# Opening the SSD stage while the last half sums run, and putting the dt products behind the column tiles in the first-phase blocks, in a two-layer hybrid kernel

## The chip, the cores and the metric

The kernel runs on one core of one Trainium2 chip. The metric is the device time of one execution in microseconds (us); lower is better. Engines are named as the profile names them: PE (TensorE, matmuls), DVE (VectorE), ACT (ScalarE), POOL (GpSimd) and SP (SyncE, which here issues nearly all DMAs).

## The reference, cut to what matters

Three tiles of 128 tokens (one of context, two of latents) pass through two layers. Layer 0 is the one the change touches. Its input is normalised and modulated, and one wide projection feeds two mixers; mixer B is a bidirectional Mamba-2 scan (SSD).

```python
ss, scs, gs = modulation(c, mod_w[layer], mod_b[layer])       # Linear(SiLU(cond)), split in three
hs = rms_norm(xs, norm_pre[layer]) * (1 + scs) + ss
...
p = h @ w_in                                                  # u, v, za | z | x, B, C | dt
...
xbc = jax.nn.silu(depthwise_conv(xbc, conv_w, conv_b))        # 5 taps, centred
dt = jax.nn.softplus(dt_raw.reshape(b, n, 2, B_HEADS) + dt_bias)
a = -jnp.exp(a_log)
y_f, h_f = ssd_scan(xs, dt[:, :, 0], a[0], bm, cm, h0_f)
y_b, h_b = ssd_scan(flip(xs), flip(dt[:, :, 1]), a[1], flip(bm), flip(cm), h0_b)
y = y_f + flip(y_b) + (d_skip[0] + d_skip[1])[:, None] * xs
y = y.reshape(b, n, B_WIDTH) * jax.nn.silu(z)
y = rms_norm(y.reshape(b, n, B_GROUPS, B_WIDTH // B_GROUPS), ...)
```

There are 32 heads of 64 channels in 8 groups, with a state of 128 and chunks of 128 tokens.

## The kernel before

Every weight is cut into units of 128 x 1024 (512 KB) in the order of use, and each float32 product is made of three matmuls: a unit is split into a high part `wh` (ACT) and the rest `wl` (DVE), the activations into `hH` and `hL`, and PE adds `hH*wh`, `hL*wh` and `hH*wl`. A list `plan` holds all units in order. SP loads them into three `raw` buffers; `wh` and `wl` have four buffers each, so a split waits until PE has used the unit four places earlier.

The order of all instructions is fixed when the program is built. A model clock (`Clock`) guesses when each engine is free; generators hold the side work (convolution, scan, gates), and after each triple of matmuls `tick()` lets those go on whose inputs the clock holds ready. At the end `in_order` ties each engine to that written order. On the chip nothing is moved: an instruction that waits holds up all that stand behind it on its engine.

**First phase (the `while` loop after `x_in`).** The modulation weights come in eight blocks `b` of eight units. `mod_pair` multiplies two units by the condition (rows `sm<-aL,sc` and `sm<-wide,sc`); after the fourth pair ACT copies the sum (`rb`), PE makes columns of it (`sm<-sel,rb`), and DVE and ACT make two more 128-row blocks of `hb`, `hH` and `hL`, the modulated input. Only then can products with these rows start. One unit per block, `part`, holds the weights of four column tiles (group 0 of x, B and C); its products go to the four banks of `first`. One unit holds all weights of dt, split into `dth`; its products go to a fifth bank, `dt_ps`. Ten units called `half` are half sums of later column tiles (groups 1 to 3), rows `sm<-hH,wh` and the like; they need the first four blocks and are parked in SBUF rows `r`.

**SSD stage.** `dt_gen` turns `dt_ps` into decays; `conv_gen(g, i)` runs the convolution of column tile `i` (0, 1: x, 2: B, 3: C) of group `g`; `ssd_gen` is the scan, `decay_gen` the decay matrices (rows `EE`, `cb`), `gate_gen` the gate and the norm of one group. Meanwhile PE makes the projections of the next columns. PSUM has eight banks: five for products (`mm`), three for the side work (`sm`). A product needs a free `mm` bank:

```python
pss = [bank() for _ in range(NT)]        # three banks: the z columns of two groups
xstat(pss, hH, hL, k1=8)                 # first half of the rows
xbc(2 * q)                               # four column tiles, one bank each
xstat(pss, hH, hL, k0=8)                 # second half
spawn(zs_gen(q, pss))
xbc(2 * q + 1)
```

The bank of a column tile is free when `conv_gen` has copied it out (rows `xpad<-mm,r` on DVE or `xpad<-mm` on ACT). The three z banks are free when `zs_gen` has read them (ACT `zs<-mm`, then DVE `zs<-zs,mm`); `zs` has one buffer, so this waits until the gate of the group before has made its last product with the old `zs` (DVE `v<-v,zs`) and ACT has taken its square (`tmp,ss<-v`). Column tile `i` of group `g` is called (g, i) below. Groups 0 to 3 with q up to 1 are the part that matters here.

Of the kernel before, what the change touches and what calls it, by code (L numbers as in the profile page):

```python
# [16 lines left out]
P = 128  # L17
# [158 lines left out]
def build(tc, A, O):  # L176
# [5 lines left out]
    with ExitStack() as ctx:  # L182
# [223 lines left out]
        for b in range(8):  # L406
            many, at = SIDE.get(b, (0, 0))
            for u in range(8):
                if b > 0 and u == at:
                    if b == 1:  # L410
                        job(("dt",), "w", "win0", 0)
                    job(("part", b - 1), "w", "win0", b)
                    for _ in range(many):
                        job_half()
                job(("mod", b, u), "raw", "mod0", 8 * b + u)
# [158 lines left out]
        convw = pd.tile([P, 32, 6], F32, name="convw")  # L574
        st = ExitStack()
# [112 lines left out]
        def weights(n):  # L688
# [13 lines left out]
            if what[0] == "part":  # L702
                hv = h.rearrange("p (k i c) -> p k i c", k=2, i=4)
                lv = l.rearrange("p (k i c) -> p k i c", k=2, i=4)
                for kk in range(2):
                    k = 2 * what[1] + kk
                    q.append((k, (dthl[:, k],), lambda k=k: dt_one(k)))
                    for i in range(4):
                        q.append(product(first[i][:, :T], hv[:, kk, i], lv[:, kk, i], k, k == KC - 1))
                q.append((None, (), close_w))  # L710
            else:
# [20 lines left out]
        def ready(item):  # L732
            k, aps, _ = item
            if k is None:
                return 0.0
            if k // 2 not in rows_of_h:
                return None
# [31 lines left out]
        while mod_at or w_at or rb or any(queue.values()):  # L769
# [22 lines left out]
            if what == "x":  # L792
                x_transpose(*xts.pop(0))
                if not xts:
                    stx.close()
                    wide = pool("wide", 1, st=stx, side="right").tile([P, 6, UNIT], F32, name="wide")
                    more += [wide[:, i] for i in range(6)]
                    dt_ps = bank()
                    first = [bank() for _ in range(4)]
            elif what == "rb":  # L800
# [3 lines left out]
                if b == 1:  # L804
                    SP.dma_start(out=convw, in_=A["convw"])
            elif what == "mod":
# [22 lines left out]
        assert len(part) == len(half) + 4 and not held.keys() & set(range(phase))  # L829
        state["next"] = phase  # L830
# [17 lines left out]
        dsk2 = pd.tile([P, 2, 32], F32, name="dsk2")  # L848
        dsk = pd.tile([P, 32], F32, name="dsk")
        arow = pd.tile([P, 64], F32, name="arow")  # L850
        dtb = pd.tile([P, 64], F32, name="dtb")
        S.dma_start(out=dsk2, in_=A["dskip"].partition_broadcast(P))
        S.dma_start(out=arow, in_=A["alog"].partition_broadcast(P))
        S.dma_start(out=dtb, in_=A["dtbias"].partition_broadcast(P))
# [338 lines left out]

        spawn(dt_gen())
        for i in range(4):
            spawn(conv_gen(0, i, None))
        spawn(ssd_gen())
# [695 lines left out]
```

## Time and profile before

| | us |
|---|---|
| median of three runs | 1825.82 (1821.43 to 1825.92) |
| the profiled execution, its own time | 1825.12 |
| its span, first to last instruction | 1823.3 |
| PE busy in the span | 1771.7 (97%) |
| DVE, ACT, POOL busy | 1258.9, 739.5, 202.2 |

The span is divided by the profile into busy and idle time of each engine, and idle time is put down to the engine or the DMA that ended it. Since PE is busy for 97% of the span, what counts is the 51.6 us in which it is not. All instructions are recorded by one helper, so the line is L155 everywhere, and rows are told apart by their tiles.

### The profile page before, as it was taken

How to read it: one execution, taken by the hardware profiler on the slowest of the kernel's cores; microseconds unless marked ns; L12 is line 12 of the kernel's file. 1: busy time of each engine (PE TensorE's matmuls, PEld its weight loads, DVE VectorE, ACT ScalarE, POOL GpSimd, SP SyncE). 2: the span in 40 equal slices, each digit the busy share in tenths (PEclk: the TensorE clock that was granted, in tenths of full speed). 3: DMA queues.
4: the chain of work that ended last, by engine and by line, in shares of the span. 5: the costliest groups of instructions: out<-in, count | busy, mean ns of one | idle time of the engine just before them, and what ended most of it. 6: DMA issues, size and time to landing. Idle time of an engine off the chain costs nothing.

```text
span 1823.3 us, 24950 instructions
## 1 busy us (share of the span) xinstructions
PE 1771.7 (97%) x9319; PEld 1542.9 (85%) x9319; DVE 1258.9 (69%) x2024; ACT 739.5 (41%) x1380; POOL 202.2 (11%) x247
## 2 busy tenths in 40 slices
PE   6899999999999999999999999998999999999998
PEld 3579888989998788889999999877789898988876
DVE  4335787787668777777888788666477676876444
ACT  3224665565543422333333323245434444444441
POOL 0000242243211000000000000021301010000000
PEclk9999999999999999999999999999999999999999
DMA  9883555455434565676666666685464444444483
GB/s 358 349 317 118 177 156 157 137 153 166 133 116 152 183 217 169 221 223 207 202 215 202 198 210 206 206 255 193 136 196 151 144 148 136 152 141 140 148 274 116
DMA packets 109896, 340.89 MB, mean 187 GB/s; under 512 B 11984, under 2 KB 29904, under 8 KB 108624
## 3 DMA queue, kind: packets, MB, share of 16 engines
q1 hardware_dynamic: 109248, 339.18, 56.9%
q8 instruction: 73, 1.20, 0.3%
q14 instruction: 47, 0.39, 0.1%
q10 hardware_dynamic: 528, 0.13, 0.0%
HBM read 330.22 MB, written 9.04 MB: 186 GB/s over the span
## 4 chain that ended last, share of the span: by engine, by line
PE 67%; DVE 5%; DMA 3%; ACT 2%; issue 2%; POOL 1%; DVEq 0%; POOLq 0%; ACTq 0%; SPq 0%
PE mm L155 62%; PE sm L155 5%; DMA raw<-in_wout_dram 2%; DVE wl L155 1%; DVE acc L155 1%; ACT jk L155 1%; ACT wh L155 1%; DVE hb L155 1%; DVE v L155 1%; DMA raw<-in_mod_dram 0%; DVE out L155 0%; DMA gn<-gate 0%; DVE cs L155 0%; DMA raw<-in_win_dram 0%; ACT xn L155 0%
## 5 line engine op out<-in xcount | busy, mean ns | idle before, releaser
L155 DVE TENSOR_TENSOR wl<-raw,wh 128x1024 fp32r<-128x1024 f32 x358 | 439.6, 1235 | 297.1 <-ACT wh L155 294.9
L155 ACT ACTIVATE wh<-raw 128x1024 fp32r<-128x1024 f32 x358 | 376.0, 1056 | 489.5 <-DMA raw<-in_win_dram 205.7
L155 PE MATMUL mm<-hH,wh 128*128 128x384 f32 x1200 | 422.3, 352 | 4.2 <-DVE xpad L155 4.2
L155 PE MATMUL mm<-hH,wl 128*128 128x384 f32 x1200 | 403.8, 337 | 1.4 <-DVE wl L155 1.4
L155 PE MATMUL mm<-hL,wh 128*128 128x384 f32 x1200 | 403.1, 336 | 0.0
L155 DVE SCALAR_TENSOR_TENSOR acc<-raw,scol,acc 128x512 f32<-128x512 f32 x480 | 336.8, 762 | 12.8 <-DMA raw<-in_mod_dram 12.5
L155 PE MATMUL mm<-wh,hH 128*128 128x512 f32 x636 | 261.5, 411 | 0.8 <-ACT v L155 0.8
L155 PE MATMUL mm<-wh,hL 128*128 128x512 f32 x636 | 248.9, 391 | 0.6 <-POOL hL L155 0.6
L155 PE MATMUL mm<-wl,hH 128*128 128x512 f32 x636 | 248.1, 390 | 0.0
L155 PEld LDWEIGHTS mm<-hH,wh 128*128 128x128 f32 x1200 | 226.5, 189 | 23.1 <-issue 20.6
L155 PEld LDWEIGHTS mm<-hH,wl 128*128 128x128 f32 x1200 | 226.2, 189 | 2.4 <-DVE wl L155 2.4
L155 PEld LDWEIGHTS mm<-hL,wh 128*128 128x128 f32 x1200 | 226.7, 189 | 1.9
L155 PE MATMUL mm<-wh,aL 128*128 128x512 f32 x504 | 197.1, 391 | 0.0
L155 PEld LDWEIGHTS mm<-wh,hL 128*128 128x128 f32 x636 | 119.3, 188 | 26.9 <-POOL hL L155 1.1
L155 PEld LDWEIGHTS mm<-wh,hH 128*128 128x128 f32 x636 | 119.6, 188 | 25.7 <-ACT v L155 1.3
L155 PEld LDWEIGHTS mm<-wl,hH 128*128 128x128 f32 x636 | 119.8, 188 | 24.0
L155 PE MATMUL mm<-wh,r 128*128 128x512 f32 x348 | 136.9, 393 | 0.5 <-DVE out L155 0.5
L155 PE MATMUL mm<-wl,r 128*128 128x512 f32 x348 | 136.2, 391 | 0.9 <-DVE wl L155 0.9
L155 POOL TENSOR_TENSOR rs_r<-rs_t,nhalf 128x1 f32<-128x1 f32 (+1 forms) x54 | 43.0, 798 | 648.1 <-DVE rs_t L155 648.1
L155 PEld LDWEIGHTS mm<-wh,aL 128*128 128x128 f32 x504 | 95.0, 189 | 19.9
L155 DVE SCALAR_TENSOR_TENSOR cv<-xpad,convw,cv 128x386 f32<-128x386 f32 x128 | 84.3, 662 | 2.3
L155 PEld LDWEIGHTS mm<-wh,r 128*128 128x128 f32 x348 | 65.3, 188 | 16.3 <-issue 2.1
(256 smaller groups left out, 2074.8 us busy)
## 6 DMA issues: line engine op xcount, KB each, us to landing
raw<-in_win_dram SPq DMA_DIRECT2D x273, 512.0 KB, 4.0
raw<-in_mod_dram SPq DMA_DIRECT2D x128, 512.0 KB, 4.1
raw<-in_wout_dram SPq DMA_DIRECT2D x104, 512.0 KB, 4.2
aL<-in_mod_dram SPq DMA_DIRECT2D x52, 512.0 KB, 7.8
cb<-cumd SPq DMA_DIRECT2D x32, 384.0 KB, 5.2
wide<-in_mod_dram SPq DMA_DIRECT2D x12, 512.0 KB, 9.9
gn<-gate SPq DMA_DIRECT2D x8, 512.0 KB, 7.0
x<-in_x_dram SPq DMA_DIRECT2D x3, 1024.0 KB, 7.3
```

Source lines behind the costliest of these rows:

```text
L155: i = f(*a, **kw)
```

## The change

Three things move. (1) In the first block the unit of `part` is loaded and split ahead of that of dt, and in every block the eight column products of the unit stand ahead of the two dt products. (2) The loop of the first phase becomes a function, `phase_job`. It runs alone until only half sums are left; then the pools of the SSD stage are opened, `dt_gen` and the convolutions of group 0 are started, and the remaining half sums are made with a `tick()` after each job. (3) Three small loads (`dskip`, `alog`, `dtbias`) go from ACT's queue at the start of the SSD stage to SP's queue after the fifth block. No product, split or copy is added or taken away.

```diff
                 if b > 0 and u == at:
+                    job(("part", b - 1), "w", "win0", b)
                     if b == 1:
                         job(("dt",), "w", "win0", 0)
-                    job(("part", b - 1), "w", "win0", b)
...
                 for kk in range(2):
                     k = 2 * what[1] + kk
-                    q.append((k, (dthl[:, k],), lambda k=k: dt_one(k)))
                     for i in range(4):
                         q.append(product(first[i][:, :T], hv[:, kk, i], lv[:, kk, i], k, k == KC - 1))
                 q.append((None, (), close_w))
+                for kk in range(2):
+                    k = 2 * what[1] + kk
+                    q.append((k, (dthl[:, k],), lambda k=k: dt_one(k)))
...
-        while mod_at or w_at or rb or any(queue.values()):
+
+        def phase_job():
+            nonlocal first, dt_ps
             pump()
...
+                if b == 4:
+                    SP.dma_start(out=dsk2, in_=A["dskip"].partition_broadcast(P))
+                    SP.dma_start(out=arow, in_=A["alog"].partition_broadcast(P))
+                    SP.dma_start(out=dtb, in_=A["dtbias"].partition_broadcast(P))
...
+        while mod_at or rb or queue["part"] or any(jobs[n][0] != "half" for n in w_at):
+            phase_job()
         st.close()
...
         spawn(dt_gen())
         for i in range(4):
             spawn(conv_gen(0, i, None))
+        while w_at or queue["half"]:
+            phase_job()
+            tick()
         spawn(ssd_gen())
         spawn(decay_gen())
```

The first place is PE in block 0, behind the first block's columns (`sel`). The dt products stand first before the change.

```order
L155 MATMUL sm_304<-sel_83,rb_298 128x2 x4
L155 MATMUL sm_319<-aL_107,sc_125 32x512 x4
L155 MATMUL mm_277<-hH_101,dth_182 128x384
L155 MATMUL mm_277<-hL_102,dth_182 64x384
L155 MATMUL mm_278<-hH_101,wh_328 128x384
L155 MATMUL mm_278<-hL_102,wh_328 128x384
L155 MATMUL mm_278<-hH_101,wl_329 128x384
```

After the change, at the same place, the column products come first (bank `mm_282` is what `mm_278` was).

```order
L155 MATMUL sm_308<-sel_83,rb_302 128x2 x4
L155 MATMUL sm_323<-aL_107,sc_129 32x512 x4
L155 MATMUL mm_282<-hH_101,wh_330 128x384
L155 MATMUL mm_282<-hL_102,wh_330 128x384
L155 MATMUL mm_282<-hH_101,wl_331 128x384
L155 MATMUL mm_283<-hH_101,wh_330 128x384
```

All four column tiles and a pair of modulation units are now done before dt's first product, which moved some 30 matmuls down; in the later blocks too the dt products stand behind.

The second place is ACT where the first phase ends. Before the change ACT copies two of the `first` banks (`r1`, `r2`), goes on with the half sums (`r5`, `r3`), issues the three small loads, and opens the SSD stage with `arow` and the copy of `dt_ps` (`EE<-mm`).

```order
L155 ACTIVATE r2_672<-mm_280 128x384
L155 ACTIVATE wh_1149<-raw_1018 128x1024
L155 ACTIVATE r5_675<-sm_1092 128x384
L155 ACTIVATE wh_1163<-raw_1065 128x1024
L155 ACTIVATE r3_673<-sm_1162 128x384
L155 ACTIVATE wh_1195<-raw_1097 128x1024
L155 ACTIVATE r3_673<-sm_1194 128x384
L155 DMA dsk2_1240<-in_dskip_dram 128x64
L155 DMA arow_1242<-in_alog_dram 128x64
L155 DMA dtb_1243<-in_dtbias_dram 128x64
L155 ACTIVATE arow_1242<-arow_1242 128x64
L155 ACTIVATE EE_1272<-mm_277 128x384
```

After it the opening stands right behind the copies, with the first convolutions (`cv`).

```order
L155 ACTIVATE r2_679<-mm_284 128x384
L155 ACTIVATE arow_123<-arow_123 128x64
L155 ACTIVATE EE_1186<-mm_281 128x384
L155 ACTIVATE cv_1191<-xpad0_1176,convw_120 128x386
L155 ACTIVATE cv_1195<-xpad1_1177,convw_120 128x386
L155 ACTIVATE r5_682<-sm_1099 128x384
L155 ACTIVATE wh_1202<-raw_1072 128x1024
L155 ACTIVATE EE_1185<-EE_1185 128x192
L155 ACTIVATE r3_680<-sm_1201 128x384
```

On PE the first small products of dt (`sm<-EE`) moved with it: they stood behind the first 33 z products, and now stand ahead of the last 33 half-sum matmuls.

The third place is DVE and ACT at the column tiles of group 3, which PE makes behind the z columns of q = 1. Before the change the bank that PE takes for tile (3, 3) is that of tile (3, 1), `mm_2472`, and DVE frees it in the last row here (the z banks are `mm_1769` to `mm_1771`, and come free later).

```order
L155 SCALAR_TENSOR_TENSOR cv_2506<-xpad0_1247,convw_120,cv_2506 128x386 x2
L155 TENSOR_TENSOR v0_1231<-v0_1231,zs_1569 128x256
L155 TENSOR_TENSOR wl_2615<-raw_2443,wh_2614 128x1024
L155 SCALAR_TENSOR_TENSOR cs3_2644<-cs3_2644,cv_2361 128x128
L155 SCALAR_TENSOR_TENSOR cs3_2644<-cs3_2644,cv_2361 128x256
L155 TENSOR_TENSOR xpad1_1248<-mm_2472,r3_673 128x256
```

After the change PE takes the first z bank, `mm_1801`, for tile (3, 2), and the wait built into its first matmul `mm_2613<-hH_101,wh_2395` is for the last of these DVE rows; between the last matmul of tile (3, 1) and that one no PE instruction stands in the program.

```order
L155 TENSOR_TENSOR tmp_2526<-sm_2523,ec_1174 128x512
L155 TENSOR_TENSOR v0_1167<-v0_1167,tmp_2526 128x256 x2
L155 TENSOR_SCALAR v0_1167<-v0_1167,rs_r_2437 128x256
L155 TENSOR_TENSOR v0_1167<-v0_1167,sm_2540 128x256
L155 TENSOR_TENSOR v0_1167<-v0_1167,zs_1624 128x256
L155 SCALAR_TENSOR_TENSOR cv_2462<-xpad1_1177,convw_120,cv_2462 128x386 x2
L155 TENSOR_TENSOR v0_1167<-v0_1167,zs_1624 128x256
L155 TENSOR_TENSOR EE_2497<-EE_2497,cb_2329 128x3x128
L155 SCALAR_TENSOR_TENSOR cv_2390<-xpad0_1176,convw_120,cv_2390 128x386 x2
L155 TENSOR_TENSOR EE_2497<-EE_2497,cb_2421 128x3x128
L155 TENSOR_TENSOR v0_1167<-v0_1167,zs_1624 128x256
L155 SCALAR_TENSOR_TENSOR zs_2610<-zs_2610,mm_1801 128x512
```

ACT's rows of the same stretch stand like this; DVE's last row above needs the `zs<-mm` in the last row here.

```order
L155 ACTIVATE wh_2514<-raw_2354 128x1024
L155 ACTIVATE tmp_2554,ss_2553<-v0_1167 128x256
L155 ACTIVATE tmp_2563,ss_2562<-v0_1167 128x256
L155 ACTIVATE EE_2497<-cb_2421,bj_1172 128x128 x3
L155 ACTIVATE cb_2421<-cb_2421,bj_1172 128x128 x3
L155 ACTIVATE r0_2589<-sm_2585,vec_84 128x384
L155 ACTIVATE EE_2497<-cb_2498,bj_1172 128x128 x3
L155 ACTIVATE cb_2498<-cb_2498,bj_1172 128x128 x3
L155 ACTIVATE tmp_2608,ss_2607<-v0_1167 128x256
L155 ACTIVATE zs_2610<-mm_1801 128x512
```

So the eviction of the z columns moved ahead in the program, from behind tile (3, 3) to in front of tile (3, 2), and the scan, gate and decay work that it needs moved with it. From the end of the SSD stage on, PE's order is the same in both programs.

## Rows read from the trace of the kernel before

**Rows 1.** Waits of PE over the whole span: us in total, times, longest

```profile
PE mm L155 <- DVE xpad L155: 4.2, 3, 2.6
PE mm L155 <- DVE dth L155: 3.6, 1, 3.6
...
PE sm L155 <- DVE v L155: 0.8, 1, 0.8
```

**Rows 2.** Busy time by stretch: length, then PE, PEld, DVE, ACT, POOL, clock, DMA

```profile
75.00:175.00 100.00, 99.71 (x576) 80.01 (x577) 35.90 (x60) 31.12 (x44) 2.02 (x6) 0.99 0.66 242
```

**Rows 3.** Timeline of PE, block 0: start, length, row, idle time before it

```profile
33.16 0.69 PE L155 MATMUL mm<-hH,dth 128*128 128x384 f32 x1 [3.58 <-DVE dth L155]
```

**Rows 4.** Timeline of ACT, block 0

```profile
30.81 1.04 ACT L155 ACTIVATE dth<-raw 128x1024 fp32r<-128x1024 f32 x1
```

**Rows 5.** Timeline of DVE, block 0

```profile
31.88 1.23 DVE L155 TENSOR_TENSOR dth<-raw,dth 128x1024 fp32r<-128x1024 f32 x1
33.02 1.22 DVE L155 TENSOR_TENSOR wl<-raw,wh 128x1024 fp32r<-128x1024 f32 x1
```

**Rows 6.** Timeline of PE, block 3

```profile
72.62 0.44 PE L155 MATMUL mm<-hH,dth 128*128 128x384 f32 x1 [1.68 <-ACT hH L155]
...
74.83 0.69 PE L155 MATMUL mm<-hH,wl 128*128 128x384 f32 x1 [0.48 <-DVE wl L155]
```

**Rows 7.** Timeline of PE, starts of tiles (2,3), (3,0), (3,2), (3,3)

```profile
252.75 0.41 PE L155 MATMUL mm<-hH,wh 128*128 128x384 f32 x1 [0.52 <-DVE xpad L155]
...
279.23 0.53 PE L155 MATMUL mm<-hH,wh 128*128 128x384 f32 x1
...
291.05 0.41 PE L155 MATMUL mm<-hH,wh 128*128 128x384 f32 x1 [1.12 <-DVE xpad L155]
...
303.09 0.49 PE L155 MATMUL mm<-hH,wh 128*128 128x384 f32 x1 [2.58 <-DVE xpad L155]
...
304.98 1.98 PE L155 MATMUL sm<-cm,cs 128*128 128x128 f32 x9
```

**Rows 8.** Busy time by stretch behind the start of tile (3,3), columns as in rows 2

```profile
303.00:305.00 2.00, 1.91 (x7) 1.85 (x8) 0.28 (x1) 1.66 (x2) 0.00 (x0) 0.57 0.58 234
...
307.00:309.00 2.00, 2.00 (x13) 2.00 (x12) 0.00 (x0) 2.00 (x7) 0.00 (x0) 1.00 0.86 271
```

**Rows 9.** Timeline of PE, first z product and dt's first small products

```profile
164.79 0.39 PE L155 MATMUL mm<-wh,hH 128*128 128x512 f32 x1
...
172.32 0.78 PE L155 MATMUL sm<-EE 128*128 128x64 f32 x6
```

**Rows 10.** Timeline of DVE ahead of tile (3,3), to the release of the z banks

```profile
296.34 0.54 DVE L155 TENSOR_TENSOR EE<-EE,cb 128x384 f32<-128x384 f32 x1
296.81 0.41 DVE L155 TENSOR_TENSOR v<-v,zs 128x256 f32<-128x256 f32 x1
297.14 1.26 DVE L155 SCALAR_TENSOR_TENSOR cv<-xpad,convw,cv 128x386 f32<-128x386 f32 x2
298.32 0.42 DVE L155 TENSOR_TENSOR v<-v,zs 128x256 f32<-128x256 f32 x1
300.32 1.23 DVE L155 TENSOR_TENSOR wl<-raw,wh 128x1024 fp32r<-128x1024 f32 x1 [1.58 <-ACT wh L155]
...
310.16 0.69 DVE L155 SCALAR_TENSOR_TENSOR zs<-zs,mm 128x512 f32<-128x512 f32 x1 [3.40 <-ACT zs L155]
```

**Rows 11.** Timeline of ACT in the same stretch

```profile
294.32 0.97 ACT L155 ACTIVATE EE<-cb,bj 128x128 f32<-128x128 f32 x3
295.20 0.97 ACT L155 ACTIVATE cb<-cb,bj 128x128 f32<-128x128 f32 x3
...
298.83 0.42 ACT L155 ACTIVATE tmp<-v 128x256 bf16<-128x256 f32 x1 [1.07 <-DVE v L155]
...
299.25 1.04 ACT L155 ACTIVATE wh<-raw 128x1024 fp32r<-128x1024 f32 x1
```

**Rows 12.** One tile's instructions: DVE rows that read xpad, ns shortest/median/longest

```profile
L155 DVE SCALAR_TENSOR_TENSOR cv<-xpad,convw,cv x128: 522/621/977, 173.8 to 562.3; 128x386 f32<-128x386 f32 x128
```

More of the change, by code (lines that the diff above doesn't have):

```diff
@@ L574, in build @@
         convw = pd.tile([P, 32, 6], F32, name="convw")
+        dsk2 = pd.tile([P, 2, 32], F32, name="dsk2")
+        dsk = pd.tile([P, 32], F32, name="dsk")
+        arow = pd.tile([P, 64], F32, name="arow")
+        dtb = pd.tile([P, 64], F32, name="dtb")
         st = ExitStack()
@@ L735, in ready @@
                 return 0.0
+            if "dt" in [jobs[n][0] for n in w_at] and aps and aps[0].name == dthl.name:
+                return None
             if k // 2 not in rows_of_h:
@@ L796, in build @@
                     wide = pool("wide", 1, st=stx, side="right").tile([P, 6, UNIT], F32, name="wide")
-                    more += [wide[:, i] for i in range(6)]
+                    more.extend(wide[:, i] for i in range(6))
                     dt_ps = bank()
@@ L828, in build @@
                         free()
-        assert len(part) == len(half) + 4 and not held.keys() & set(range(phase))
-        state["next"] = phase
+        while mod_at or rb or queue["part"] or any(jobs[n][0] != "half" for n in w_at):
+            phase_job()
         st.close()
@@ L847, in build @@
         tot = pd.tile([P, NT, 64], F32, name="tot")
[L848 to L854, printed above, removed]
         xpad = [pw.tile([P, PADW], F32, name=f"xpad{i}") for i in range(2)]
@@ L1196, in build @@
             spawn(conv_gen(0, i, None))
+        while w_at or queue["half"]:
+            phase_job()
+            tick()
+        assert len(part) == len(half) + 4 and not held.keys() & set(range(phase))
+        state["next"] = phase
         spawn(ssd_gen())
```

## The prediction

> **What bounds the kernel.** I read the share of each engine first: PE is busy for 1771.7 of 1823.3 us, so the program is as long as PE's work plus the 51.6 us in which PE stands still, and only what adds to or takes from that idle time (or slows PE's clock) can move the end. The second view is the list of PE's waits. It names no DMA: PE waits for copies and splits on DVE and ACT [rows 1]. The third is the pace of PE where nothing holds it: 576 matmuls, nearly all of 384 columns, in 99.71 us at a granted clock of 0.99 [rows 2], so 0.173 us each. The changed program has the same matmuls, and from the end of the SSD stage on they stand in the same order. I therefore count only waits ahead of that point: the wait for dt's split (3.6 us) and those for `xpad` copies (4.2 us in three) with the small one for `v` (0.8 us), and any new wait.
>
> **Term a: the first phase, +0.4 us.** In block 0, PE stands idle for 3.58 us until 33.16, for dt's split [rows 3]. ACT's first split there starts at 30.81 and takes 1.04 [rows 4], and DVE's two follow at 31.88 and 33.02 [rows 5], 1.14 apart. With `part` first, the same two engines make the same splits in the other order. PE can then start two products (those with `wh`) at about 31.9, but the next needs `wl`, which is where dt's was, at 33.1. So the wait changes its name, and some 0.6 us of work is pulled ahead of it. I give no credit for that: the next block's products wait for the modulated rows, which come from the modulation chain and not from this unit, so PE only waits that much longer there. Blocks 1 to 7 already have their order of loads; there only PE's order changes. Behind block 3, PE started dt's products at 72.62, after 1.68 us for `hH`, and still waited 0.48 for `wl` at 74.83 [rows 6]: the two dt matmuls (2 x 0.173 = 0.35 us) lay inside a wait that ends with `wl` in any case. After the change they stand behind, so the wait is 0.35 longer and they cost their time later: +0.35, rounded with some slack to +0.4. Bounds: -1.7 if the 0.6 us head start keeps PE's clock up in block 0, +1.5 if a longer idle in block 1 takes it down once more; both sizes are what half clock costs in term b.
>
> **Term b: waits that go, -6.7 us.** Four waits belong to the old order of banks and convolutions: 0.52, 1.12 and 2.58 us at the starts of tiles (2,3), (3,2) and (3,3) [rows 7], and 0.8 for `v` [rows 1]: 5.0. The last of the three costs more than itself. Behind it six matmuls take from 303.09 to 304.98, 1.89 us [rows 7], where 6 x 0.173 = 1.04 is usual, and the nine small ones behind them 1.74 instead of some 0.9 (an estimate from half of it). The granted clock there is 0.57, and 1.00 again from 307 [rows 8]: 1.2 instead of 2.4 GHz. That is 0.85 + 0.85 = 1.7 us. All of it goes if the SSD stage is far enough ahead when PE comes there.
>
> How far ahead is it? Everything of it is opened while 33 matmuls of half sums and the 33 first z products are still to be made. The z products took from 164.79 to 172.32 [rows 9], 7.5 us, the half sums 33 x 0.173 = 5.7: a head start of 13.2 us for the side work.
>
> **Term c: waits that come, +9.7 us.** The head start makes the banks turn differently. Two places are left where PE meets a bank that is not yet free.
>
> At tile (2,3), PE takes the bank of the `xpad` copy as before. One split and one gate product more stand ahead of that copy on DVE now; I put the wait at 0.9 (before 0.52), with 0 and 1.7 (the 0.52 and one split, 1.14) as its ends.
>
> At tile (3,2), PE takes a z bank, since the program has its release in front. I walk there, with zero at the start of tile (3,1) on PE.
> - PE: (3,0) and (3,1) with the small products took from 279.23 to 289.93 (291.05 less the wait of 1.12), 10.7 us, of which 48 x 0.173 = 8.3 are tile products [rows 7]. Tile (3,1) alone is 24 x 0.173 = 4.15 and some 2.4 of small products: PE is through at 6.5, and nothing else stands in its program before the z bank.
> - DVE: by laying its rows out one behind the other I have it at the copy of the last bank of group 2 until -2.0. Then come two splits (1.14), two pairs of convolution products (297.14 to 298.32, 1.18), one `EE` product (296.34 to 296.81, 0.47), `tmp` (as the z eviction, 0.69) and six products of `v` (296.81 to 297.14, 0.33) [rows 5, 10]: 2.3 + 2.4 + 0.5 + 0.7 + 2.0 = 7.8. A split waits for ACT's half, as at 300.32, where that was 1.58 [rows 10]; I take 1.9 for both. The second gate product is there at 7.7.
> - ACT: then the square of `v` (0.42), twelve exponentials (294.32 to 295.20 is 0.88 for three, so 3.5), a copy of 128 x 384 (0.5, estimate from the 0.42 of 128 x 256), the last square (0.42) and the z activation (0.5, estimate likewise) [rows 11]. An engine keeps its order: at 298.83 ACT waited 1.07 for `v`, with a split behind it that needed no `v` [rows 11]. ACT is done at 7.7 + 5.3 = 13.0.
> - DVE's `zs` product takes 0.69 [rows 10]: the bank is free at 13.7, and PE has waited **7.2 us**.
>
> A second way to the same: before, the z banks came free at 310.16 + 0.69 = 310.85 [rows 10], 19.8 us after (3,2) had started at 291.05 [rows 7]. Less 13.2 of head start that is 6.6. The walk is the finer of the two and I keep 7.2. Its ends: 5.3 if the splits never wait for ACT (7.2 - 1.9), 9.3 if DVE runs as it does in its slow rows, 977 ns for a convolution product instead of 621 (0.36 more for each of four, and the rest in proportion) [rows 12].
>
> PE stands for 7.2 us, so I expect the half clock behind it as behind the 2.58 [rows 8], and put it at 1.5. The Trainium skill ("TensorE: Matmul & The Clock Gate", Part 1, What's actually happening) says that the throttled state is the default and that activity releases it. It speaks against this change, which swaps three short stops for one long one: by it the long stop is sure to cost a restart. It also says that there are only two rates, so that the length of the stop should not matter to the price, and that leaves the sum as it is; were the price in proportion to the stop (1.7 x 7.2 / 2.58 = 4.7), the sum would be 3.2 higher. No run here shows yet which. In all 0.9 + 7.2 + 1.5 = 9.6, and 0.1 for a short new wait in group 3's last tiles: +9.7. Behind the stall the side work has caught up, so I charge nothing at (3,3).
>
> **The small loads, 0.** Three DMA issues leave ACT, 1.4 us there by the gaps in its timeline, which was not awaited by PE; SP gets them behind the fifth block, where its own queue waits for free buffers and PE waits for no DMA. If SP's issues did delay a weight by their 1.4 us, PE would have to be short of weights, which no row of [rows 1] shows.
>
> **Sum.** 1825.12 (the profiled execution's own time, 0.7 under the median) + 0.4 - 6.7 + 9.7 = 1828.5; with the 0.7 to the median, **1829 us**. Some 0.3%, 5.5 us, is about what a measurement of this kernel can tell from no change.
>
> **Rivals.**
> 1. *The stage is early enough, and nothing waits at (3,2):* 1825.8 + 0.4 - 6.7 + 0.9 = 1820. It decides at 6.5 us behind the start of (3,1): the gate's last square must be done 7 us sooner than in my walk. For it speaks that the walk adds one engine's rows behind the other's, and that the two copies of work on ACT might be done while DVE is waiting; against it that twelve exponentials stand on ACT ahead of the release in the order printed above, and the second way (19.8 less 13.2). 0.10.
> 2. *The stall is longer:* DVE shares its time with POOL's work and runs at its slow rows, 9.3, the clock price is the proportional one or a second restart follows: 1829 + 2.1 + 1 to 3 = 1832 to 1834. For it: 977 ns in [rows 12]; against: the median of 621 holds for most. 0.25.
> 3. *The first phase decides:* a kept clock in block 0 (-1.7) with a stall at its low end (5.3): 1829 - 1.7 - 1.9 = 1825.4, no change at all. 0.10.
> 4. My forecast, 1829, with its own range of 1826 to 1831: 0.55.
>
> Faster by over 0.3% (below 1820.3) takes the lower half of rival 1 and a little of 3: 0.10. Slower by over 0.3% (above 1831.3) takes rival 2: 0.27. Within: 0.63. The range reaches from rival 1's time to past rival 2's: 1820 to 1835.
>
> **What would show it.** In the changed kernel's waits of PE: no `xpad` wait above 1 us, and one new wait of a product for DVE's `zs`, 5 to 9 us, at the start of tile (3,2), with a clock near half behind it. ACT's rows ahead of it should be twelve exponentials between two squares of `v`. In block 0 the wait for dt's split becomes one for `wl` of about 1.2 us behind two products, and behind block 3 the wait for `wl` grows by 0.35. If the `zs` wait is under 2 us, the walk has failed at the order of ACT or at the head start; if it is there and the time is still lower, the price of term b was too small.

## The result, and the profile after

The changed kernel took 1836.32 us (median of four runs, 1835.19 to 1838.64) against 1825.87 before: a ratio of 1.0061, 95% interval 1.0049 to 1.0073, so 0.6% or some 10.5 us slower. The forecast was 1829, range 1820 to 1835. The profiled execution has a span of 1835.2 us (1823.3 before). PE made the same 9319 matmuls in it and was busy 2.1 us longer (1773.8 against 1771.7):

```profile
PE 1773.8 (97%) x9319; PEld 1545.8 (84%) x9319; DVE 1261.6 (69%) x2024; ACT 738.7 (40%) x1380; POOL 206.9 (11%) x247
```

Waits of PE over the whole span (us in total, times, longest), changed kernel; the lines that stand where [rows 1] stood:

```profile
PE mm L155 <- ACT wh L155: 9.2, 6, 2.5
PE mm L155 <- DVE zs L155: 8.4, 1, 8.4
PE mm L155 <- DVE wl L155: 4.9, 9, 0.8
...
PE mm L155 <- ACT tmp L155: 3.4, 1, 3.4
...
PE sm L155 <- DVE v L155: 0.9, 1, 0.9
```

No row of the list names dt's split or an `xpad` copy on DVE any more. The 9.2 us for `wh` are no loss of that size: most of them lie in the first phase, where PE now waits for the split of the unit of `part` instead of for dt's split (3.6 us before), `hH` (2.7) and `hL` (1.7). New are a stop of 8.4 us for the z columns and one of 3.4 us that the list puts down to ACT's `tmp`. Where these two are, in the timeline of PE (start, length, row, idle time before it):

```profile
259.73 0.41 PE L155 MATMUL mm<-hH,wh 128*128 128x384 f32 x1 [3.40 <-ACT tmp L155]
...
262.54 1.80 PE L155 MATMUL sm<-xb,xw 128*128 128x128 f32 x8
264.10 0.42 PE L155 MATMUL mm<-hH,wh 128*128 128x384 f32 x1
...
298.88 0.33 PE L155 MATMUL sm<-cm,v 128*128 128x128 f32 x1 [0.89 <-DVE v L155]
307.56 0.69 PE L155 MATMUL mm<-hH,wh 128*128 128x384 f32 x1 [8.35 <-DVE zs L155]
...
311.57 0.49 PE L155 MATMUL mm<-hH,wh 128*128 128x384 f32 x1
```

The row at 259.73 is the start of tile (2,3), that at 307.56 the start of tile (3,2). Behind each the granted clock is down (length, PE, PEld, DVE, ACT, POOL, clock, DMA):

```profile
260.00:265.00 5.00, 5.00 (x25) 4.96 (x24) 3.14 (x6) 3.40 (x9) 1.23 (x2) 0.66 0.46 157
305.00:310.00 5.00, 2.44 (x8) 2.44 (x9) 2.92 (x4) 3.70 (x10) 0.00 (x0) 0.50 0.25 34
```

Behind (3,2) twelve matmuls take 4.01 us (307.56 to 311.57) where 12 x 0.173 = 2.08 is usual: 1.9 us lost. Behind (2,3) six take 1.96 us instead of 1.04 and eight small ones 1.56 (262.54 to 264.10) where the next eight of their kind take 0.81 (335.87 to 336.68): 1.7 lost.

What ended the stop at (3,2), on DVE and ACT of the changed kernel:

```profile
299.08 0.42 DVE L155 TENSOR_TENSOR v<-v,zs 128x256 f32<-128x256 f32 x1
...
300.60 0.74 DVE L155 TENSOR_TENSOR v<-v,zs 128x256 f32<-128x256 f32 x1
...
303.78 0.80 DVE L155 TENSOR_TENSOR EE<-EE,cb 128x384 f32<-128x384 f32 x1 [0.46 <-POOL cb L155]
304.50 0.41 DVE L155 TENSOR_TENSOR v<-v,zs 128x256 f32<-128x256 f32 x1
306.82 0.69 DVE L155 SCALAR_TENSOR_TENSOR zs<-zs,mm 128x512 f32<-128x512 f32 x1 [1.90 <-ACT zs L155]
```

```profile
301.85 0.97 ACT L155 ACTIVATE EE<-cb,bj 128x128 f32<-128x128 f32 x3
302.72 0.97 ACT L155 ACTIVATE cb<-cb,bj 128x128 f32<-128x128 f32 x3
303.60 0.56 ACT L155 ACTIVATE r<-sm,vec 128x384 fp32r<-128x384 f32 x1
304.06 0.97 ACT L155 ACTIVATE EE<-cb,bj 128x128 f32<-128x128 f32 x3
304.94 0.97 ACT L155 ACTIVATE cb<-cb,bj 128x128 f32<-128x128 f32 x3
305.81 0.40 ACT L155 ACTIVATE tmp<-v 128x256 bf16<-128x256 f32 x1
...
306.21 0.57 ACT L155 ACTIVATE zs<-mm 128x512 f32<-128x512 f32 x1
```

The third product of `v` is there at 304.9, but ACT is in its twelve exponentials until 305.8: the picture of the walk. The product itself stands behind an `EE` product that takes ACT's second three exponentials as its input (in the program `EE_2497<-EE_2497,cb_2421`; the list names POOL). At tile (2,3) it is DVE that stands, twice, for ACT:

```profile
253.73 0.73 DVE L155 SCALAR_TENSOR_TENSOR r<-r,cv 128x128 f32<-128x128 f32 x2 [2.33 <-ACT r L155]
...
256.66 1.64 DVE L155 TENSOR_TENSOR wl<-raw,wh 128x1024 fp32r<-128x1024 f32 x1 [1.52 <-ACT wh L155]
258.22 0.83 DVE L155 TENSOR_TENSOR v<-v,zs 128x256 f32<-128x256 f32 x1
258.97 0.61 DVE L155 TENSOR_TENSOR xpad<-mm,r 128x128 f32<-128x128 f32 x2
```

```profile
251.65 0.97 ACT L155 ACTIVATE EE<-cb,bj 128x128 f32<-128x128 f32 x3
252.53 0.97 ACT L155 ACTIVATE cb<-cb,bj 128x128 f32<-128x128 f32 x3
253.41 0.60 ACT L155 ACTIVATE r<-cv 128x128 f32<-128x128 f32 x2
```

The copy at 258.97 ends some 0.2 us before PE goes on at 259.73, so the list's "ACT tmp" is a row that happened to end then: by the program the first matmul of (2,3) waits for that copy. It is an `xpad` wait after all, 3.40 us long.

### The profile page after: what moved, and what is told of

Its sections match the earlier page's. It is cut to its first block, busy times and chain, and to the rows that moved or that the text cites. A ratio compares the mean times of both kernels' runs of the same rounds, so it can differ in the third digit from the quotient of the medians.

```text
span 1835.2 us, 24961 instructions
## 1 busy us (share of the span) xinstructions
PE 1773.8 (97%) x9319; PEld 1545.8 (84%) x9319; DVE 1261.6 (69%) x2024; ACT 738.7 (40%) x1380; POOL 206.9 (11%) x247
## 4 chain that ended last, share of the span: by engine, by line
PE 87%; DVE 6%; ACT 3%; DMA 2%; issue 2%; POOL 0%; DVEq 0%; SPq 0%; POOLq 0%; ACTq 0%
PE mm L155 76%; PE sm L155 11%; DVE wl L155 1%; DVE hb L155 1%; DVE v L155 1%; ACT wh L155 1%; DVE acc L155 1%; DMA raw<-in_wout_dram 1%; DMA raw<-in_mod_dram 0%; ACT hH L155 0%; DMA gn<-gate 0%; DVE cs L155 0%; ACT jk L155 0%; DMA x<-in_x_dram 0%; ACT rb L155 0%
## 5 line engine op out<-in xcount | busy, mean ns | idle before, releaser
L155 PEld LDWEIGHTS mm<-wl,r 128*128 128x128 f32 x348 | 65.4, 188 | 16.0 <-DVE wl L155 3.0
```

The costliest lines, as they stand in the source:

```text
L155: i = f(*a, **kw)
```

## The experiments

All ratios are to the kernel before on the same chip, with 95% intervals. The theory at the start (A) was that both parts cost: the first phase through longer idle pieces and a falling clock, the opening through the two stops.

**The two big parts apart.** `e1_dt_behind`: the kernel before with part (1) alone.

```diff
+                    job(("part", b - 1), "w", "win0", b)
                     if b == 1:
                         job(("dt",), "w", "win0", 0)
-                    job(("part", b - 1), "w", "win0", b)
...
-                    q.append((k, (dthl[:, k],), lambda k=k: dt_one(k)))
...
+                    q.append((k, (dthl[:, k],), lambda k=k: dt_one(k)))
```

> The kernel before with the first-phase order of the change alone (part ahead of dt, the dt products behind the column products, the SSD stage opened as before). Theory A, from the trace of the changed kernel: without the two dt products PE has nothing to do between hH and the split of the unit of part in blocks 1 to 3, waits 1.0 to 2.2 us in one piece, and its clock falls to half behind some of these waits where before it did not; 2 to 4 us slower than the kernel before (1828 to 1830), with a granted clock near 0.5 behind block 1 and block 2. Theory B, term a of the prediction: one wait 0.35 us longer, 0.4 us slower, the clock of blocks 1 and 2 stays at 1.0. The waits on xpad of the SSD stage (0.5, 1.1, 2.6 us) stay in both.

Measured: 1827.08 us, ratio 1.0006 (0.9997 to 1.0014), 1 us and not to be told from nothing. Theory A fell on the time, though the waits were there as it said (1.77, 0.97 and 2.18 us before blocks 1 to 3, clock 0.52 at 49 to 51 us).

`e2_open_early`: the changed kernel with both edits of part (1) undone.

```diff
-                    job(("part", b - 1), "w", "win0", b)
                     if b == 1:
                         job(("dt",), "w", "win0", 0)
+                    job(("part", b - 1), "w", "win0", b)
```

> The changed kernel with dt loaded and multiplied ahead of part again, so that only the early opening of the SSD stage and the small loads on SP are left. Theory A: the two long stalls at tiles (2,3) and (3,2), 3.4 and 8.4 us and half clock behind each, belong to the opening; 7 to 9 us slower than the kernel before (1833 to 1835), 2 to 4 us faster than the change. Theory B: the first phase is harmless (0.4 us) and all of the loss is the opening's; 10 to 11 us slower, the same as the change.

Measured: 1838.19 us, 1.0068 (1.0055 to 1.0081). The loss is the opening's and the loads'. The stop at (3,2) is there, but for another bank, that of tile (3,0):

```profile
308.11 0.66 PE L155 MATMUL mm<-hH,wh 128*128 128x384 f32 x1 [7.00 <-DVE xpad L155]
```

So it is not the z bank as such that is late.

`e3_dt_behind_block0` (the changed kernel, dt products behind in the first block alone):

```diff
+                    if what[1] > 0:
+                        q.append((k, (dthl[:, k],), lambda k=k: dt_one(k)))
                     for i in range(4):
                         q.append(product(first[i][:, :T], hv[:, kk, i], lv[:, kk, i], k, k == KC - 1))
                 q.append((None, (), close_w))
-                for kk in range(2):
+                for kk in range(2 * (what[1] == 0)):
```

> The changed kernel with the dt products behind the column products in the first block alone; in the seven later blocks, where the split of dt is long there, they stand ahead again. The order of loading stays as changed. Theory A (the lost cover behind hH is what drops the clock): 2 to 4 us faster than the change, 1832 to 1834, clock 1.0 behind blocks 1 and 2, waits for wh gone there. Theory B (order of loading, or chance of the clock at the start): no different from the change, 1836.

Measured: 1842.76 us, 1.0092 (1.0078 to 1.0105): slower than the change, against both. `e9_block0_alone` put the same first phase on the kernel before (that edit with that of e1):

> The kernel before with the order of loading of the change, and dt behind the column products in the first block alone: the first phase of e3 with the old opening. e3 was 4.5 us slower than e2, which differ in this alone. Theory A (the first block's order costs this in itself, by a clock that falls there and stays low): 3 to 5 us slower than before, 1829 to 1831, with more half clock before 100 us. Theory B (it costs nothing alone, and e3's loss came about with its SSD order): within 1.5 us of before.

Measured: 1827.79 us, 1.0012 (1.0002 to 1.0022). Alone it costs some 2 us (0.4 to 4.0). The SSD stage of e3 does not explain the rest: its stops at tiles (2,2), (2,3) and (3,2) are 1.54, 1.54 and 6.62 us, those of e2 2.18, 1.61 and 7.00, and from the first z product to the end the two traces differ by 0.6 us (1672.6 and 1672.0). What e3 has over e2 came ahead of that, 2.2 us in these single traces and 4.6 between the medians, and its cause stays open.

**How much a first phase differs by itself.** `e12_before_again` is the kernel before, with no edit.

> The kernel before once more, as a control and for a second trace of it: within 0.5 us of its other runs. Its half clock and idle time between 28 and 160 us show how much the first phase differs between two executions of one program: if by 1.5 us or more, the 3 us between single traces of the old and the new first phase are no measure of the change's own cost; if by less than 0.5, they are.

Measured: 1826.67 us, 0.9997 (0.9988 to 1.0005). Its first z product starts 2.2 us after that of [rows 9], though the program is the same:

```profile
167.03 0.39 PE L155 MATMUL mm<-wh,hH 128*128 128x512 f32 x1
```

In the changed kernel it starts at 167.76, in e1 at 167.37. One trace of each is no measure of part (1); the medians of e1 are. From that product to the end of the span the changed kernel takes 1667.4 us, against 1658.5 and 1659.1 in the two traces of the kernel before and 1658.1 in e1: the loss lies behind the first phase.

**What the stops hang on.** `e4_exps_held` (the changed kernel, exponentials of one head and its followers held behind the z columns), and `e5_exps_held_both` (six more of them held behind the last convolution of group 1). In `decay_gen`:

```diff
+                while n == 7 and ("conv", 1, 3) not in flags:    # e5 only
+                    yield
+                while n == 13 and ("zs", 1) not in flags:        # e4 and e5
+                    yield
                 load(n + 2)
                 mask(n + 1)
```

> The changed kernel with the exponentials of one head and its followers held back in the program until the z columns of q = 1 are copied out, so that the twelve exponentials that stood on ACT between two squares of v are behind the release of the z banks. Theory A (the walk: ACT's order sets the end of the stall): the wait at tile (3,2) shrinks from 8.4 by about 3.5 to some 5 us, and the time by 3 to 3.5, to 1833, if the exponentials do not make a wait later. Theory B (DVE, which POOL and the splits hold up, is late anyway): the wait stays within 1 us of 8.4 and the time at 1836.

> As e4_exps_held, and the six exponentials that stood on ACT ahead of the last convolution of group 1 are held back behind it too, so that DVE is not held up ahead of the copy of tile (2,1). Theory A (both stalls end with DVE, which waits for ACT behind exponentials): the wait at tile (2,3) falls from 3.4 to under 2, the half clock behind it goes, and the time is 2 to 4 us under that of e4, 1830 to 1832. Theory B (the copy is late because DVE has too much ahead of it, whatever ACT does): the wait stays at 3 and the time at that of e4, 1834.

Measured: e4 1833.80 us, 1.0044 (1.0030 to 1.0057), the stop at (3,2) 5.47 instead of 8.35. ACT now stands for the third product of `v`:

```profile
304.94 0.42 ACT L155 ACTIVATE tmp<-v 128x256 bf16<-128x256 f32 x1 [0.82 <-DVE v L155]
```

e5 1829.63 us, 1.0019 (1.0010 to 1.0028), with these stops on PE at (2,3) and (3,2):

```profile
259.18 0.41 PE L155 MATMUL mm<-hH,wh 128*128 128x384 f32 x1 [2.26 <-ACT tmp L155]
```

```profile
299.93 0.69 PE L155 MATMUL mm<-hH,wh 128*128 128x384 f32 x1 [4.26 <-DVE zs L155]
```

Twelve exponentials take 3.5 us on ACT (301.85 to 303.60 and 304.06 to 305.81 in the changed kernel). With them and what hangs on them written behind the release, 2.9 us of the stop are gone, as A said, and DVE's rows are what is left; in e5 DVE works without a pause from 283.6 to 297.8. At (2,3) e5's stop is 2.26 (A: under 2), and no half clock follows it. Writing these rows elsewhere, with the early opening kept, thus leaves 3.3 us of the 10.5. What e5 still loses agrees with its stops: 1.1 for the first phase, -6.7 for the waits that went, 2.26 + 4.26, and 2.7 of half clock behind the second make 3.6.

`e6_six_banks` (the change) and `e10_before_six_banks` (the kernel before) take one PSUM bank from the side work:

```diff
-MM = 5
+MM = 6
```

> The changed kernel with six PSUM banks for products and two for the side work instead of five and three, so that tile (3,2) gets a bank that is free long before. Theory A (the loss is the release of a bank): no wait over 2 us between 240 and 330, and 8 to 14 us faster than the change (1822 to 1828). Theory B (the side work itself is late, and PE meets it at its next small product if not at the bank): the stall moves to a small product or to the next tile, and the time stays within 4 us of 1836.

> The kernel before with six PSUM banks for products and two for the side work: the control of e6. Theory A: the waits on xpad copies (0.5, 1.1, 2.6 us and 1.7 of half clock) go, 4 to 6 us faster than before (1820 to 1822), so that with six banks the early opening is worth about nothing or up to 3 us. Theory B: with two banks the side work is slower and PE waits for it elsewhere; 0 to 5 us slower than before.

Measured: e6 1835.17 us, 1.0056 (1.0043 to 1.0070); e10 1850.72 us, 1.0133 (1.0117 to 1.0150). Theory A of both (a gain) fell. In e6 nothing waits at (3,2); the z banks are waited for where the next z columns need them, and two banks for the side work make stops in the first phase too, for a bank that ACT must empty:

```profile
107.04 1.80 PE L155 MATMUL sm<-aL,sc 128*32 128x512 f32 x8 [1.89 <-ACT r L155]
...
320.97 0.50 PE L155 MATMUL mm<-wh,hH 128*128 128x512 f32 x1 [2.48 <-DVE zs L155]
```

The stop needs the shortage of banks; a sixth is no cure.

`e7_open_dt_only` starts the convolutions behind the half sums, dt's decays ahead; `e11_gate_together` writes the three gate products of group 1 together, on top of e5 (with n = 7 held until `("cs", 1, 0)`).

```diff
         spawn(dt_gen())
-        for i in range(4):
-            spawn(conv_gen(0, i, None))
         while w_at or queue["half"]:
             phase_job()
             tick()
+        for i in range(4):
+            spawn(conv_gen(0, i, None))
```

```diff
-                yield y
+                if g != 1 or t == 0:
+                    yield (ys[0], ys[1], ys[2]) if g == 1 else y
```

> The changed kernel in which only dt's decays are started while the last half sums run, and the convolutions of group 0 behind them. In its program tile (3,2) takes a z bank as in the change. Theory A (the convolutions set the head start of the scan, and the stall goes by how much of the scan and gate is written ahead of the z release): still a wait for zs at (3,2), 6 to 10 us, and slower than before by 7 to 12 us. Theory B (the early convolutions are what displaces the work): back within 3 us of the kernel before.

> The changed kernel with two of the decay steps held back as in e5, and the three gate products of group 1 written together once all three inputs are there. In its program the z banks come free behind tile (3,3) again, as before the change, and (3,2) and (3,3) take the banks of (3,0) and (3,1). Theory A (the early start is worth what term b said, and only the place of the release spoiled it): no wait over 1.5 us from 240 to 330, 2 to 6 us faster than before (1820 to 1824). Theory B (DVE is full in this stretch, so that a wait of 3 us or more stays at one of these tiles): 1 us faster to 4 us slower than before.

Measured: e7 1833.59 us, 1.0036 (1.0023 to 1.0049), stops of 3.22 at (2,3) and 7.41 at (3,2); e11 1830.12 us, 1.0020 (1.0011 to 1.0028), stops of 4.61 at (3,2) and 2.25 at (3,3), now for `xpad` copies. Less head start gives the same stop; putting the z release back behind (3,3) does too, for another row. Term b's gain did not come without a stop elsewhere in any of these.

**The three small loads.** `e8_loads_on_sp`: the kernel before with part (3) alone.

```diff
+                if b == 4:
+                    SP.dma_start(out=dsk2, in_=A["dskip"].partition_broadcast(P))
+                    SP.dma_start(out=arow, in_=A["alog"].partition_broadcast(P))
+                    SP.dma_start(out=dtb, in_=A["dtbias"].partition_broadcast(P))
...
-        S.dma_start(out=dsk2, in_=A["dskip"].partition_broadcast(P))
-        S.dma_start(out=arow, in_=A["alog"].partition_broadcast(P))
-        S.dma_start(out=dtb, in_=A["dtbias"].partition_broadcast(P))
```

> The kernel before with the three small loads on SP behind the fifth block, alone. Theory A (as predicted, hidden): within 1 us of the kernel before. Theory B (they delay weights on SP's queue or are part of the opening's loss): 2 us or more slower.

Measured: 1835.88 us, 1.0054 (1.0036 to 1.0071): three loads of 32 KB, and 9.6 us. PE stops at four tiles in it, for 2.00 us at (2,2), 2.55 at (2,3), and then at (3,2) and (3,3):

```profile
299.78 0.66 PE L155 MATMUL mm<-hH,wh 128*128 128x384 f32 x1 [2.85 <-DVE xpad L155]
```

```profile
317.32 0.66 PE L155 MATMUL mm<-hH,wh 128*128 128x384 f32 x1 [4.46 <-DVE xpad L155]
```

Its program has another order in the SSD stage: a load issued from ACT moves the builder's model of ACT and of the DMA forward, and without it the side work is dealt out otherwise. Two kernels take that apart. `e13_loads_same_order` issues the loads on SP and tells the model clock of them as before; `e14_order_alone` does the reverse.

```diff
+                if b == 4:                                       # e13; e14: clock.note("SP", ...) here
+                    nc.sync.dma_start(out=dsk2, in_=A["dskip"].partition_broadcast(P))
...
+        for o, i in ((dsk2, "dskip"), (arow, "alog"), (dtb, "dtbias")):   # e14: nc.scalar.dma_start here
+            clock.note("S", "dma_start", (), {"out": o, "in_": A[i].partition_broadcast(P)})
```

> The kernel before with the three small loads on SP behind the fifth block, but with the builder's model clock told of them where and as before, so that the rows of PE, DVE and POOL stand exactly as before and those of ACT too, but for the three loads. Theory A (what e8 lost is the order that the builder wrote after the move): within 1.5 us of the kernel before. Theory B (the loads themselves cost it, on SP or by late data): 8 to 10 us slower, as e8.

> The reverse of e13: the order of e8 on PE, DVE, POOL and ACT to the row, with the three loads left on ACT where they were. Theory A: 8 to 11 us slower than before, as e8, with the same four xpad waits. Theory B: within 1.5 us of before.

Measured: e13 1824.95 us, 0.9997 (0.9986 to 1.0007); e14 1837.62 us, 1.0063 (1.0046 to 1.0081), with stops of 2.21, 2.69, 2.85 and 4.39 at the same four tiles. The loads cost nothing; the order written after them costs all of it.

**The opening without the loads' move.** `e15_opening_alone` (old first phase) and `e16_no_loads_moved` (new first phase) issue the loads from ACT where the stage opens:

```diff
-                if b == 4:
-                    SP.dma_start(out=dsk2, in_=A["dskip"].partition_broadcast(P))
...
+        S.dma_start(out=dsk2, in_=A["dskip"].partition_broadcast(P))
```

> The early opening alone: dt first in the first phase as before, the three loads on ACT where the stage opens. Theory A (a head start of the side work spoils the order at tiles (2,3) and (3,2) in itself): 7 to 13 us slower than before, with a wait of 5 us or more at (3,2). Theory B (the loss of e2 came with the loads' move): within 4 us of before.

> The change without its third part: new first phase, early opening, the three loads on ACT where the stage opens. Theory A: as the change within 3 us, 1833 to 1839. Theory B: within 4 us of the kernel before, 1824 to 1830.

Measured: e15 1840.56 us, 1.0074 (1.0062 to 1.0087); e16 1843.84 us, 1.0093 (1.0080 to 1.0106), both more than theory A had. The early opening costs by itself, and the parts do not add up: moving the loads costs 9.6 us alone and gives some 7 back inside the change (17.6 us over its kernel before in e16, 10.5 in the change). The stop of e15 at (3,2):

```profile
310.56 0.69 PE L155 MATMUL mm<-hH,wh 128*128 128x384 f32 x1 [12.31 <-DVE zs L155]
```

**The same reading used on the kernel before.** There, (3,3) waits 2.58 us for a copy on DVE that has two gate products, a decay product and a split ahead of it, and the split waits for ACT behind a square [rows 10, 11]. `e17_gate_behind_copy` writes the gate of group 1 behind that copy; `e18_gate_and_exps_behind` writes six exponentials and their followers behind it too.

```diff
+            flags.add(("xp", g, i))                              # in conv_gen, behind the copy
...
-            while ("zs", g // 2) not in flags:
+            while ("zs", g // 2) not in flags or g == 1 and ("xp", 3, 1) not in flags:
...
+                while n == 12 and ("xp", 3, 1) not in flags:     # e18 only, in decay_gen
+                    yield
```

> The kernel before with the gate of group 1 written behind the copy of tile (3,1), so that neither a gate product on DVE nor a square on ACT stands ahead of the copy that tile (3,3) waits for. Theory A (the written order ahead of the release sets the wait): the wait of 2.6 to 3.1 us at (3,3) falls to 1 to 1.5, the half clock behind it may go; 1 to 3 us faster than before, if the z banks, which come later, are not awaited. Theory B (DVE has more than PE's tile takes in any order, or the z banks become the wait): within 1 us of before or slower.

> As e17, and the six exponentials and the decay product ahead of the copy are written behind it too. Theory A: the wait at (3,3) is under 0.7 us, no half clock there, 2 to 5 us faster than before (1821 to 1824). Theory B: a wait of the same size comes at the z banks or at a later tile, and the time stays within 1 us of before.

Measured: e17 1822.20 us, 0.9980 (0.9971 to 0.9990), with no wait left at (3,3), where its theory A had 1 to 1.5 us, but a new one of 0.56 us at the z columns behind it; e18 1819.95 us, 0.9966 (0.9953 to 0.9978), 5.6 us faster than before on the same chip (1825.57) and the best of all kernels here. In e18's timeline tile (3,3) starts without a wait, and the small products behind its first two triples run at the full clock:

```profile
301.09 0.33 PE L155 MATMUL mm<-hH,wh 128*128 128x384 f32 x1
...
302.13 1.14 PE L155 MATMUL sm<-cm,cs 128*128 128x128 f32 x9
303.03 0.43 PE L155 MATMUL mm<-hH,wh 128*128 128x384 f32 x1
```

The nine small matmuls take 1.14 where [rows 7] had 1.98 at half clock. A gain of 2.6 to 3.1 us of wait (two traces of the kernel before) and 1.7 of clock, 4.3 to 4.8, agrees with the 5.6 within the interval (4.0 to 8.6). The same sum holds for e17, where only its new 0.56 goes off, and there 3.4 were measured (1.8 to 5.3).

## Why the prediction was wrong, step by step

The sign in its likeliest case and the place of the loss were right, the size was not. Its sum with what was measured for each term, as far as single traces can tell:

| term | predicted | measured |
|---|---|---|
| a, first phase | +0.4 | +1.1 (e1, interval -0.5 to +2.6) |
| b, waits that go | -6.7 | -6.7: none of them is left in its old size and place |
| c, tile (2,3) | +0.9 | +3.4, and 1.7 of half clock behind it |
| c, tile (3,2) | +7.2 | +8.35, and 0.89 for `v` at the small product before it |
| c, half clock behind (3,2) | +1.5 | +1.9 |
| c, later tiles | +0.1 | +0.6 (one `xpad` wait behind group 3, at 369.15) |
| sum on 1825.8 | 1829 | 1837.1 (measured 1836.3) |

The sum is no finer than its terms: a is known to some 1.5 us, and the four waits of b came to 6.4 us instead of 5.0 in e12, the second trace of the kernel before.

**The step that failed** is the one on tile (2,3): "One split and one gate product more stand ahead of that copy on DVE now; I put the wait at 0.9", with 1.7 as its upper end. It was 3.4, and 5.1 with the half clock behind it, for which the prediction had nothing at this tile: 4.2 of the 7.3 us by which the forecast was short. I counted what had been added to DVE's rows and did not walk ACT, as I did for (3,2). Ahead of the copy DVE stood for 2.33 us for `r` and 1.52 for `wh`, 3.85 together, because ACT had six exponentials ahead of `r` and a square ahead of `wh`; with the exponentials moved (e5) the stop was 2.26 and the clock stayed up. With its upper end and a clock price, which I had only given to the longer stop, the sum would have been 1831.5; with a walk that finds the 3.4, some 1833.

**Tile (3,2).** The head start was there: ACT's copy of `dt_ps`, among the first rows of the stage, stood 4.2 us behind the first z product before the change and 9.9 ahead of it after, 14.1 us where the prediction had 13.2.

```profile
168.96 0.47 ACT L155 ACTIVATE EE<-mm 128x384 f32<-128x384 f32 x1
```

```profile
157.88 0.49 ACT L155 ACTIVATE EE<-mm 128x384 f32<-128x384 f32 x1 [0.58 <-PE mm L155]
```

The walk was right as a mechanism (e4: without the exponentials 2.9 us less) and 1.2 short in size, inside its own bounds of 5.3 to 9.3. Tile (3,1) started at 291.69. PE was through 7.5 us later (6.5 in the walk, the 0.89 for `v` between), the second gate product was done at 9.6 (301.3; 7.7 in the walk), and from there to the end of the z activation (306.78) ACT took 5.5 (5.3 in the walk). So the error lay with DVE: its copy of the last bank of group 2 ended 0.7 us ahead of the tile and not 2.0, and the rows behind it were 0.6 slower.

**The clock.** The price of 1.5 for the long stop was near the 1.9 measured; in proportion to the stop it would have been 5.5 behind 8.35. But a fixed price per stop is not what the runs show either. The Trainium skill ("TensorE: Matmul & The Clock Gate", Part 1, What's actually happening) has only two rates, and the steps of the 384-column matmuls agree with that: 0.32 us at half clock, 0.173 at full clock. How long the half clock lasted did not follow the stop. Behind 3.22 us at (2,3) of e7 there was none:

```profile
256.29 0.41 PE L155 MATMUL mm<-hH,wh 128*128 128x384 f32 x1 [3.22 <-DVE xpad L155]
```

```profile
256.00:261.00 5.00, 4.71 (x26) 4.45 (x27) 3.21 (x8) 2.50 (x5) 0.99 (x2) 1.00 0.19 48
```

Behind the 4.26 us of e5, 17 matmuls took 5.60 us (299.93 to 305.53) where 17 x 0.173 = 2.94 is usual, 2.7 lost. Behind 11.99 us at (3,2) of e16, twelve took 3.93 (313.94 to 317.87) instead of 2.08, 1.9 lost (the end of e5's row of 17, then e16's lines):

```profile
305.53 0.35 PE L155 MATMUL mm<-hH,wl 128*128 128x384 f32 x1
```

```profile
313.94 0.69 PE L155 MATMUL mm<-hH,wh 128*128 128x384 f32 x1 [11.99 <-DVE zs L155]
...
317.87 0.49 PE L155 MATMUL sm<-cm,v 128*128 128x128 f32 x3
```

With the 1.7 behind 2.58 and 3.40, the 1.9 behind 8.35 and some 3 behind the 12.31 of e15, the price lay between nothing and 3 us, and not in the order of the lengths. That 1.5 came close here is in part luck; what sets it was not found.

**Term a** is not contradicted in size (1.1, with an interval of -0.5 to 2.6), but its picture was off. In block 0 PE waited 2.46 us for `wh` and 0.25 for `wl`, not 1.2 for `wl`, and the clock was kept up no more than before (0.72 in both from 28 to 40 us). Behind block 1 it fell, as the upper bound had it (0.52 at 49 to 51 us, 1.00 before).

**The small loads** cost nothing on the chip, as predicted (e13). That their move also re-deals the order of the stage was not told apart in the prediction, which took the whole order of the changed program as one; alone it is worth 9.6 us (e8, e14).

**The rivals.** The first (early enough, no stall) was wrong at its point of decision: the release came 8.35 us too late. The third needed a clock kept up in block 0, which did not come. The second (a longer stall, a second restart of the clock) is what happened, by a second stop more than by a longer one. It had 1832 to 1834 and a chance of 0.25; the range ended at 1835 because no case had both stops.

**The signs.** The stop for `zs` at (3,2), the half clock behind it and the twelve exponentials between two squares came as announced. "No `xpad` wait above 1 us" did not: the 3.40 at (2,3) is one, under another name in the list.

**What caused the loss,** then: the side work's written order around two tiles. A head start did not help, since DVE and ACT must do their rows in the order written, and in the programs with the early opening more of the side work was written ahead of a release that PE waits for. That the order is what costs is shown in the changed kernel by e4 and e5 (same early opening, 7.8 and 3.3 us of the 10.5 left), in the kernel before by e13 and e14 (loads moved and order kept, nothing; loads kept and order changed, 11 us), and by e17 and e18 in the other direction. Why the builder writes a worse order after an earlier opening, whatever the rest of the edit (e2, e7, e15, e16), was not settled; no kernel here changed the rule by which it deals.

## What to carry to other kernels

Where a program's order is dealt out by a model, an edit is first of all another deal: compare the rows ahead of each release that the busy engine waits for, on every engine in that chain, before pricing the edit itself, and test an edit once with the old order of all instructions kept. A stop can cost more than its length: here the half clock behind it cost between nothing and 3 us more, so two short bad places can cost more than they look. And the cheapest gain is often to write work that nobody waits for, here a gate and six exponentials, behind the copy for which the busy engine stands.

## What the runs showed of the hardware

The same program differs from execution to execution in its first 165 us by 2.2 us (164.79 and 167.03 at the first z product), with equal medians. Another difference stands ahead of any block: eight small matmuls at some 18 us took 1.87 us in the profiled execution of before, 1.59 in e12, the same program, and 1.06 in that of the changed kernel, while the clock column shows 1.00 in all three. What set that is open, and it does not explain the 2.2 us, since the slower of the two executions of before had the earlier first z product. A weight split on DVE, 1.22 us as a rule, took 1.64 at 256.66 in the changed kernel while POOL multiplied (256.60 to 258.77); no run was made to tell that apart.
